# Norm factors computed with tokens on partitions, a reordered end of two projections, and a folded pool bias and scale

## The chip, the cores and the metric

The kernel runs on one core of a Trainium2 chip. The metric is the device time of one execution in microseconds. TensorE is called PE here, its weight load PEld, VectorE DVE, ScalarE ACT, GpSimd POOL; SP issues the weight DMAs.

## The reference

Two decoder layers run over 272 tokens (16 learned meta tokens and 256 positions) of width 2048. Layer 0 mixes with a Mamba-2 scan, layer 1 with causal pooling; each is followed by a SwiGLU FFN of hidden width 5632, and every sub-layer stands between two RMSNorms:

```python
def rmsnorm(x, w):
    y = x * lax.rsqrt(jnp.mean(x * x, axis=-1, keepdims=True) + EPS)
    return y * w

for i in range(DEPTH):                      # DEPTH = 2
    u = rmsnorm(h, norm_w[i, 0])
    mix = ssd_mixer(u, ...) if i % 2 == 0 else pool_mixer(u, ...)
    h = h + rmsnorm(mix, norm_w[i, 1])
    f = (silu(u2 @ w_gate[i]) * (u2 @ w_up[i])) @ w_down[i]   # u2 = rmsnorm(h, norm_w[i, 2])
    h = h + rmsnorm(f, norm_w[i, 3])
return h[:, N_META:]

def pool_mixer(u, w_group, b, scale):       # four channel groups, windows 2, 4, 8, 16
    mixed = trailing_mean(u, window of the group) - u
    return (einsum('blgc,gcd->blgd', mixed, w_group) + b) * scale
```

## The kernel before

**Panels and steps.** Activations lie with features on partitions and tokens along the free axis, so that a weight block is the stationary operand and 272 (in layer 1's FFN 256) tokens stream. A weight matrix is worked off as panels of 512 or 768 output columns; a panel has 4 or 6 PSUM accumulators (`acc_*`, six buffers in turn) and is cut into steps of one or two blocks of 128 rows. Each fp32 weight is split: ACT casts it to `whi` (L162), DVE subtracts to get `wlo` (L175), and every block takes three matmuls (L275 to L277: hi by hi, hi by lo, lo by hi). `run_stream` goes through the steps in program order: at each step it emits the cast of the step after next and, after the third accumulator, its subtraction. Within a step all accumulators take their matmuls one after another, so the four accumulators of a panel end within its last step. A panel with `late` set puts its last subtraction behind its last accumulator.

**Junctions.** Between the sub-layers stands a row of norm factors, 1/sqrt(mean square), one number per token. `SumSq` squares the tiles of the sub-layer's output `part` on ACT, adds the squares on DVE into `ssum` or multiplies them by a matrix of ones on PE (L640: the sum over the features, repeated on all 128 partitions), and `row` takes the square root on ACT (L660). `recip` inverts the 128x272 row on DVE (L664). Then the `Producer` makes the sixteen new tiles of `h` and of the next operand `uu`: for each tile a scaled copy of `part` (`tmp`, L707), the sum with `h` (L716), `uu` hi on ACT (L717), a square, and `uu` lo on DVE (L727). It runs two tiles ahead of the matmuls and its `hook` sets in the subtraction of the next weight step. `warm` issues matmuls whose result nobody reads.

There are three such places, called A, B and C below:

- **A** (about 771 to 783 us): from the SSD output projection (panel `oB3`, accumulators `acc_oB`) to the gate panel `g0_0_0` of the first FFN (`acc_g`). PE also transposes the last eight tiles of the input there (L896, L898), which ACT copies into `h` (L899).
- **B** (about 1578 to 1618): from the down projection `d0_1_3` (`acc_d`) to layer 1's pool mixer. The sixteen tiles feed four panels of four blocks: two with tokens on the output partitions (`acc_tok`, copied to `zt`), then two like the others (`acc_pool`, copied to `part` by L1013).
- **C** (about 1615 to 1640): the second norm of the pool mixer. The factor row `rb2` of the mixer's input is inverted (L664), read back through PE transposes as columns `rt` (L1020 to L1023), multiplied into six tiles of a band matrix on ACT (L1039), and into the window sums on DVE (L1057, L1062, L1069). Band matmuls give `acc_mix` (L1046 to L1049). Sixteen output tiles get bias and scale (`tile_out`, L1030 on ACT and L1032 on DVE), are squared and summed on PE, and give the factor row of the junction to the second FFN.

The order of everything here is the order in which the code emits it; each engine works off its own instructions in that order, and there is no planner at these places.

Of the kernel before, what the change touches and what calls it, by code (L numbers as in the profile page):

```python
# [15 lines left out]
P = 128  # L16
D = 2048
# [14 lines left out]
class Panel:  # L32
    def __init__(self, name, w, nk, rhs, n, evac, after=None, ncols=512, ku=4, ks=2, dup=False,
                 need=(), pre=None, prestep=None, mm=None, func=None, late=False, lazy=False, nm=None, both=None):
        self.name, self.w, self.nk, self.rhs, self.n = name, w, nk, rhs, n
        self.evac, self.after, self.ncols, self.ku, self.ks, self.dup = evac, after, ncols, ku, ks, dup
        self.func, self.late, self.lazy, self.both = func, late, lazy, both
# [30 lines left out]
def trunk_kernel(ctx: ExitStack, tc: tile.TileContext, x, meta, norm_w, w_in, conv_w, conv_b,  # L68
# [171 lines left out]

    def run_stream():
        for si, s in enumerate(steps):
# [11 lines left out]
            if p.prestep is not None:  # L254
                p.prestep(s["k0"], s["ks"], lambda si=si: emit_lo(si + 2))
            for m in range(p.nm):
                if p.mm is not None:
                    p.mm(s, m, first, last)
                else:
                    if first:  # L260
                        p.accs.append(acc_tile(p.name))
                    a = p.accs[m]
                    for j in range(s["ks"]):
                        k = s["k0"] + j
                        xh, xl = p.rhs(k)
                        wh = s["hi"][:, j, m * P:(m + 1) * P]
                        wl = s["lo"][:, j, m * P:(m + 1) * P]
                        st, en = k == 0, k == p.nk - 1
                        if p.both is not None:

                            nc.tensor.matmul(a[:, :2 * p.n].rearrange("p (a c) -> p a c", c=p.n), lhsT=wh,  # L271
                                             rhs=p.both(k), start=st, stop=False)
                            nc.tensor.matmul(a[:, p.n:2 * p.n], lhsT=wl, rhs=xh, start=False, stop=en)  # L273
                            continue
                        nc.tensor.matmul(a[:, :p.n], lhsT=wh, rhs=xh, start=st, stop=False)  # L275
                        nc.tensor.matmul(a[:, :p.n], lhsT=wh, rhs=xl, start=False, stop=False)  # L276
                        nc.tensor.matmul(a[:, :p.n], lhsT=wl, rhs=xh, start=False, stop=en)  # L277
# [4 lines left out]
                if last and p.mm is None:  # L282
# [324 lines left out]
    class SumSq:  # L607


        def __init__(self, n):  # L610
            self.n, self.acc, self.pend, self.adds, self.bank = n, None, [], [], None
# [21 lines left out]
        def push(self, keep=0, stop=False):  # L633

            while len(self.pend) > keep:
                sq = self.pend.pop(0)
                first = self.bank is None
                if first:
                    self.bank = bank("pt")
                nc.tensor.matmul(self.bank[:, :self.n], lhsT=ones[:, 0:P], rhs=sq, start=first,  # L640
# [21 lines left out]

    def recip(dst, n):
        nc.vector.reciprocal(out=dst[:, :n], in_=dst[:, :n])  # L664

    def evac_sum(pi, n):

        def evac(m, a):
            k = pi * 4 + m
            o = part[:, k, T - n:T]  # L670
            if k == 0:
                F["ss"] = SumSq(n)
            nc.vector.tensor_tensor(out=o, in0=o, in1=a[:, :n], op=ALU.add)
            F["ss"].late()
            if pi == 3:
                F["ss"].pe(o)
                if m == 0:
                    F["ss"].push_acc()
# [7 lines left out]
    def norm_row(dst):  # L686
        n = F["ss"].n
        F["ss"].row(dst)
        F["ss"].warm(WARM)
        recip(dst, n)  # L690

    class Producer:


        def __init__(self, order, l1, w1, l2, w2, n, on_pe):
            self.order, self.n, self.on_pe = order, n, on_pe
            self.a, self.b = (l1, w1), (l2, w2)
            self.ss = SumSq(n)
            self.tmps, self.made = {}, 0

        def tmp(self, i):
            if i >= KD:
# [3 lines left out]
            self.tmps[i] = t  # L706
            nc.vector.scalar_tensor_tensor(out=t, in0=part[:, k, T - n:T], scalar=nw(*self.a, k),  # L707
                                           in1=rb[:, :n], op0=ALU.mult, op1=ALU.mult)

        def make(self, i, hook):  # L710
# [5 lines left out]
            nc.vector.tensor_tensor(out=hk, in0=hk, in1=self.tmps.pop(i), op=ALU.add)  # L716
# [121 lines left out]
    def ffn(layer, n, junction, tail):  # L838
# [6 lines left out]
        for half, widths in enumerate(((6, 4, 4, 4, 6), (4, 4, 4, 4, 4))):  # L845
# [14 lines left out]
            for pi in range(4):  # L860
                w = w_down[layer][h0 * P:c0 * P, pi * 512:(pi + 1) * 512]
                if tail is None:
# [3 lines left out]
                    elif half == 1 and pi == 3:  # L866
# [9 lines left out]
                                late=half == 1 and pi == 3, pre=sqrt_table if half == 1 and pi == 3 else None))  # L876
# [474 lines left out]
```

## Time and profile before

| | us |
|---|---|
| median of 3 runs | 2399.9 (2398.23 to 2399.99) |
| the profiled execution, its own time | 2399.69 |
| its span | 2397.6 |
| PE busy | 2364.3 (99%), 16660 matmuls |
| DVE busy | 1447.8 (60%) |
| ACT busy | 1180.2 (49%) |
| DMA | 418.37 MB, 174 GB/s |

How to read it: PE is busy nearly always, so time moves only where PE stands idle, where it does work that a change takes away or adds, or where its clock is low. A busy PE includes its matmuls at either clock.

### The profile page before, as it was taken

The numbers are of one execution on the slowest core, as the hardware profiler recorded it, in microseconds if no ns is written. First come the engines' busy times: TensorE is split into PE (matmuls) and PEld (weight loads), VectorE is DVE, ScalarE is ACT, GpSimd is POOL, SyncE is SP. The second block draws the span as 40 slices with busy tenths as digits, with TensorE's granted clock in tenths as the row PEclk, the third lists the DMA queues.
The fourth block names the chain that finished last, engine by engine and source line by source line (L and its number), as shares of the span: only waits on it lengthen the run. The fifth ranks groups of instructions, "written<-read, shape, count | busy, mean of one in ns | idle before, by whom it ended". The sixth has DMA issues, their size and how long they took to land.

```text
span 2397.6 us, 39491 instructions
## 1 busy us (share of the span) xinstructions
PE 2364.3 (99%) x16660; PEld 2219.0 (93%) x16660; DVE 1447.8 (60%) x1927; ACT 1180.2 (49%) x1605; POOL 13.8 (1%) x38
## 2 busy tenths in 40 slices
PE   7999999999999999999999999999999999999998
PEld 7999999999999999999999999988888888888886
DVE  5878867647865855454445454578666554556655
ACT  6656565445654644443344443456544444444443
POOL 0000000000000000000000000010000000000000
PEclk9999999999999999999999999999999999999999
DMA  6555555555554555565555555433665655565554
GB/s 190 170 165 182 177 167 176 170 176 178 176 178 158 147 189 175 163 189 176 176 176 173 179 176 176 167 120 106 191 195 173 192 195 192 177 199 187 197 189 141
DMA packets 203825, 418.37 MB, mean 174 GB/s; under 512 B 9920, under 2 KB 10416, under 8 KB 203504
## 3 DMA queue, kind: packets, MB, share of 16 engines
q1 hardware_dynamic: 203216, 415.07, 53.9%
q8 instruction: 130, 2.13, 0.4%
q10 hardware_dynamic: 432, 0.79, 0.1%
q14 instruction: 47, 0.39, 0.0%
HBM read 413.66 MB, written 2.17 MB: 173 GB/s over the span
## 4 chain that ended last, share of the span: by engine, by line
PE 96%; DVE 2%; ACT 1%; issue 0%; DMA 0%; SPq 0%; DVEq 0%; ACTq 0%
PE acc_g L271 7%; PE acc_u L271 7%; PE acc_g L276 4%; PE acc_g L277 4%; PE acc_d L277 4%; PE acc_g L275 4%; PE acc_u L275 4%; PE acc_u L277 4%; PE acc_u L276 4%; PE acc_d L276 4%; PE acc_d L275 4%; PE acc_g L273 3%; PE acc_u L273 3%; PE acc_z L275 3%; PE acc_z L277 3%; PE acc_z L276 3%
## 5 line engine op out<-in xcount | busy, mean ns | idle before, releaser
L175 DVE TENSOR_TENSOR wlo<-raw,whi 128x1024 fp32r<-128x1024 f32 (+2 forms) x804 | 936.9, 1167 | 772.3 <-ACT whi L162 767.7
L162 ACT CAST whi<-raw 128x1024 fp32r<-128x1024 f32 (+2 forms) x800 | 803.1, 1005 | 951.6 <-PE acc_u L276 149.3
L271 PE MATMUL acc_g<-uu,whi 128*128 128x512 f32 x704 | 248.5, 396 | 2.5 <-DVE uu L727 1.3
L271 PE MATMUL acc_u<-uu,whi 128*128 128x512 f32 x704 | 247.0, 394 | 0.2 <-DVE g L789 0.2
L275 PE MATMUL acc_g<-uu,whi 128*128 128x272 f32 x704 | 204.8, 291 | 0.9 <-ACT uu L717 0.9
L277 PE MATMUL acc_g<-uu,wlo 128*128 128x272 f32 x704 | 203.8, 289 | 0.0
L276 PE MATMUL acc_g<-uu,whi 128*128 128x272 f32 x704 | 203.5, 289 | 0.1
L277 PE MATMUL acc_u<-uu,wlo 128*128 128x272 f32 x704 | 203.2, 289 | 0.0
L277 PE MATMUL acc_d<-hidhi,wlo 128*128 128x272 f32 x704 | 203.2, 289 | 0.0
L275 PE MATMUL acc_u<-uu,whi 128*128 128x272 f32 x704 | 203.1, 288 | 0.0
L276 PE MATMUL acc_u<-uu,whi 128*128 128x272 f32 x704 | 202.7, 288 | 0.0
L275 PE MATMUL acc_d<-hidhi,whi 128*128 128x272 f32 x704 | 202.3, 287 | 0.0
L276 PE MATMUL acc_d<-hidlo,whi 128*128 128x272 f32 x704 | 202.2, 287 | 0.0
L273 PE MATMUL acc_g<-uu,wlo 128*128 128x256 f32 x704 | 197.2, 280 | 0.7 <-DVE wlo L175 0.7
L273 PE MATMUL acc_u<-uu,wlo 128*128 128x256 f32 x704 | 197.0, 280 | 0.0
L271 PEld LDWEIGHTS acc_g<-uu,whi 128*128 128x128 f32 x704 | 132.1, 188 | 34.9 <-DVE ups L815 1.9
L271 PEld LDWEIGHTS acc_u<-uu,whi 128*128 128x128 f32 x704 | 132.1, 188 | 32.0 <-DVE g L789 0.6
L275 PE MATMUL acc_z<-uu,whi 128*128 128x272 f32 x512 | 150.7, 294 | 0.0
L275 PE MATMUL acc_x<-uu,whi 128*128 128x272 f32 x512 | 150.2, 293 | 0.0
L277 PE MATMUL acc_x<-uu,wlo 128*128 128x272 f32 x512 | 147.6, 288 | 0.0
L277 PE MATMUL acc_z<-uu,wlo 128*128 128x272 f32 x512 | 147.6, 288 | 0.0
L276 PE MATMUL acc_x<-uu,whi 128*128 128x272 f32 x512 | 147.4, 288 | 0.0
(384 smaller groups left out, 5250.0 us busy)
## 6 DMA issues: line engine op xcount, KB each, us to landing
raw<-in_ffn_w_down_dram SPq DMA_DIRECT2D x88, 1024.0 KB, 5.0
raw<-in_ssd_w_in_dram SPq DMA_DIRECT2D x76, 1024.0 KB, 5.3
raw<-in_ffn_w_gate_dram SPq DMA_DIRECT2D x64, 1024.0 KB, 5.2
raw<-in_ffn_w_up_dram SPq DMA_DIRECT2D x64, 1024.0 KB, 5.2
raw<-in_ssd_w_out_dram SPq DMA_DIRECT2D x32, 1024.0 KB, 5.1
raw<-in_ffn_w_gate_dram SPq DMA_DIRECT2D x32, 768.0 KB, 4.5
raw<-in_ffn_w_up_dram SPq DMA_DIRECT2D x32, 768.0 KB, 4.5
bc<-cs_dram SPq DMA_DIRECT2D x32, 272.0 KB, 6.0
```

The lines of the kernel that those rows point to most:

```text
L162: nc.scalar.copy(out=s["hi"], in_=raw)
L175: nc.vector.tensor_tensor(out=s["lo"][:, :, sl], in0=raw, in1=s["hi"].bitcast(F32)[:, :, sl], op=ALU.subtract)
L271: nc.tensor.matmul(a[:, :2 * p.n].rearrange("p (a c) -> p a c", c=p.n), lhsT=wh, rhs=p.both(k), start=st, stop=False)
L273: nc.tensor.matmul(a[:, p.n:2 * p.n], lhsT=wl, rhs=xh, start=False, stop=en)
L275: nc.tensor.matmul(a[:, :p.n], lhsT=wh, rhs=xh, start=st, stop=False)
L276: nc.tensor.matmul(a[:, :p.n], lhsT=wh, rhs=xl, start=False, stop=False)
L277: nc.tensor.matmul(a[:, :p.n], lhsT=wl, rhs=xh, start=False, stop=en)
```

## The change

1. **Norm factors with tokens on partitions.** With `cols` set, a tile of squares is the stationary operand and one column of ones streams: three matmuls 128x1 (blocks of 128, 128 and 16 tokens, or two for 256 tokens) in place of one of 128x272. `factor_cols` takes the square root and the reciprocal of 128x3 numbers and multiplies them into an identity, one block on ACT and the others on DVE; `factor_row` multiplies these diagonal blocks by ones on PE, which puts the row on all partitions (`acc_row`, in PSUM), and ACT copies it to SBUF. The first two `tmp` read it in PSUM. In `norm_row` two warm matmuls stand ahead of the row and four behind it. At A this whole helper now stands ahead of the transposes, and it had no warm matmuls there before. The factor rows `rb2` of both FFNs keep the old way.
2. **The last two steps by accumulator.** Panels `oB3` and `d0_1_3` have `major` set: in their last two steps each accumulator takes all its twelve matmuls before the next begins. Their last step emits neither a cast nor a subtraction any more; the `hook` of the `Producer` does both. The squares of the first three accumulators go to DVE sums.
3. **The pool bias and scale.** `evac_pool` applies the scale when it copies. Squares are taken straight from `acc_mix` with scale and bias in the activation; the bias is added in `tmp`, and the norm weight moves from `tmp` to the addition to `h`. The factors `rt` come from `factor_cols`, the transposes go.

```diff
             if p.prestep is not None:
-                p.prestep(s["k0"], s["ks"], lambda si=si: emit_lo(si + 2))
+                p.prestep(s["k0"], s["ks"], lambda si=si: (emit_hi(si + 2), emit_lo(si + 2)))
...
+                elif p.major and s["k0"] >= p.nk - 4:
+
+                    if s["k0"] == p.nk - 4:
+                        if m == 0:
+                            emit_hi(si + 2)
+                            emit_lo(si + 2)
+                        for t in (s, steps[si + 1]):
+                            panel_mm(p, t, m)
+                        p.evac(m, p.accs[m])
...
-                if m == 0:
+                if m == 0 and not (p.major and last):
                     emit_hi(si + 1 + LOOK)
...
-                if not p.lazy and m == (p.nm - 1 if p.late and last else min(2, p.nm - 1)):
+                if not p.lazy and not (p.major and last) and m == (p.nm - 1 if p.late and last else min(2, p.nm - 1)):
                     emit_lo(si + 1 + LOOK)
...
+                if self.cols:
+                    for i, (t0, w, _) in enumerate(self.blocks):
+                        nc.tensor.matmul(self.bank[:, i:i + 1], lhsT=sq[:, t0:t0 + w], rhs=ones[:, 0:1],
...
+        def factor_cols(self, rs):
...
+            self.push(stop=True)
+            nb = len(self.blocks)
+            nc.scalar.activation(out=rs[:, 0:nb], in_=self.bank[:, 0:nb], func=AF.Sqrt, scale=1.0 / D, bias=eps)
+            nc.vector.reciprocal(out=rs[:, 0:nb], in_=rs[:, 0:nb])
+            self.dg = F["pool"].tile([P, T], F32, name="sq", bufs=6)
+            for i, (t0, _, w) in enumerate(self.blocks):
+                o, c = self.dg[0:w, t0:t0 + w], rs[0:w, i:i + 1]
+                if i == 1:
+                    nc.scalar.activation(out=o, in_=ident[0:w, 0:w], func=AF.Copy, scale=c)
+                else:
+                    nc.vector.tensor_scalar(out=o, in0=ident[0:w, 0:w], scalar1=c, scalar2=None, op0=ALU.mult)
+
+        def factor_row(self, dst):
+
+            b = acc_tile("row")
+            for t0, _, w in self.blocks:
+                nc.tensor.matmul(b[:, t0:t0 + w], lhsT=ones[0:w, 0:P], rhs=self.dg[0:w, t0:t0 + w], start=True,
+                                 stop=True)
+            nc.scalar.copy(out=dst[:, :self.n], in_=b[:, :self.n])
+            return b
...
     def norm_row(dst):
-        n = F["ss"].n
-        F["ss"].row(dst)
-        F["ss"].warm(WARM)
-        recip(dst, n)
+
+        rs = F["pool"].tile([P, 3], F32, name="rsc")
+        F["ss"].factor_cols(rs)
+        F["ss"].warm(2)
+        b = F["ss"].factor_row(dst)
+        F["ss"].warm(WARM - 3)
+        return b
...
             if gi == 3 and k0 == 2:
-                G["prod"].ss.row(rb2)
-                recip(rb2, T)
+                G["prod"].ss.factor_cols(G["rt"])
+                for b in G["band"]:
+                    for i in range(3):
+                        nc.scalar.activation(out=b[:, i, :], in_=b[:, i, :], func=AF.Copy, scale=G["rt"][:, i:i + 1])
...
-            nc.scalar.copy(out=part[:, g * 4 + m, :], in_=a[:, :T])
+            k = g * 4 + m
+            nc.scalar.activation(out=part[:, k, :], in_=a[:, :T], func=AF.Copy, scale=col(PSC, k))
+            if g == 0 and m == 1:
+                G["prod"].ss.factor_row(rb2)
```

The order on PE at place A, before: behind the last matmuls of `acc_oB` come the sums over the squares, then the transposes of the input.

```order
L277 MATMUL acc_oB_8317<-yhi,wlo 128x272
L640 MATMUL pt<-ssum,ones 128x272
L640 MATMUL pt<-sq,ones 128x272 x4
L896 MATMUL acc_h<-ident,mr 128x16
L898 MATMUL acc_h<-ident,xr 128x128 x2
```

The same place after; `py` are warm matmuls.

```order
L257 MATMUL acc_oB_8317<-yhi,wlo 128x272
L655 MATMUL pt<-ones,ssum 128x1 x3
L655 MATMUL pt<-ones,sq 128x1 x3
L666 MATMUL py<-ones,ident 128x272 x2
L704 MATMUL acc_row<-sq,ones 128x128 x2
L704 MATMUL acc_row<-sq,ones 128x16
L666 MATMUL py<-ones,ident 128x272 x4
L953 MATMUL acc_h<-ident,mr 128x16
L955 MATMUL acc_h<-ident,xr 128x128 x2
```

The sums have become narrow, and six warm matmuls and the row now stand ahead of the transposes.

DVE at place B, before, from the last addition to `part` to the third tile of the `Producer`:

```order
L673 TENSOR_TENSOR part<-part,acc_d_1_3_16524 128x272
L175 TENSOR_TENSOR wlo<-raw,whi 128x1024
L664 RECIPROCAL rb<-rb 128x272
L707 SCALAR_TENSOR_TENSOR tmp<-part,pv,rb 128x272
...
L716 TENSOR_TENSOR h<-h,tmp 128x272
L707 SCALAR_TENSOR_TENSOR tmp<-part,pv,rb 128x272
L626 TENSOR_TENSOR ssum<-ssum,sq 128x272
L727 SCALAR_TENSOR_TENSOR uu<-h,pv,uu 128x272
```

And after:

```order
L175 TENSOR_TENSOR wlo<-raw,whi 128x1024
L719 TENSOR_TENSOR part<-part,acc_d_1_3_16546 128x272
L639 TENSOR_TENSOR ssum<-ssum,sq 128x272
L691 RECIPROCAL rsc<-rsc 128x3
L698 TENSOR_SCALAR sq<-ident,rsc 128x128
L698 TENSOR_SCALAR sq<-ident,rsc 16x16
L761 SCALAR_TENSOR_TENSOR tmp<-part,pv,acc_row 128x272
...
L761 SCALAR_TENSOR_TENSOR tmp<-part,pv,rb 128x272
L639 TENSOR_TENSOR ssum<-ssum,sq 128x272
L175 TENSOR_TENSOR wlo<-raw,whi 128x1024
L785 SCALAR_TENSOR_TENSOR uu<-h,pv,uu 128x272
```

One subtraction moved ahead of the last addition, the other from behind it into the third tile (at A the same, with 128x768); its cast stands on ACT behind that tile's `uu`.

ACT at the start of place C, after (before, the second cast and the four copies of `acc_pool` stood ahead of the bands, and the window sums read a row that DVE had inverted itself):

```order
L690 ACTIVATE rt<-pt,eps 128x3
L696 ACTIVATE sq<-ident,rt 128x128
L1042 ACTIVATE band_16835<-band_16835,rt 128x144 x3
L1042 ACTIVATE band_16843<-band_16843,rt 128x144 x3
L162 CAST whi<-raw 128x768
L1069 ACTIVATE part<-acc_pool_17188,pv 128x272
L1069 ACTIVATE part<-acc_pool_17197,pv 128x272
L706 COPY rb_90<-acc_row 128x272
```

The copy of the row that the window sums on DVE read is the last of these.

## Rows read from the trace of the kernel before

**Rows 1.** the page, busy time of the engines, share of the span and instructions

```profile
PE 2364.3 (99%) x16660; PEld 2219.0 (93%) x16660; DVE 1447.8 (60%) x1927; ACT 1180.2 (49%) x1605; POOL 13.8 (1%) x38
```

**Rows 2.** windows: stretch, its length, busy us of each engine, clock, DMA share, GB/s

```profile
782.00:795.00 13.00, 13.00 (x102) 12.92 (x102) 13.00 (x28) 9.48 (x19) 0.00 (x0) 0.99 0.41 121
...
1587.00:1600.00 13.00, 12.97 (x57) 8.94 (x57) 12.81 (x31) 9.66 (x20) 0.00 (x0) 1.00 0.18 49
1600.00:1618.00 18.00, 17.02 (x111) 14.59 (x111) 16.34 (x31) 13.70 (x30) 0.00 (x0) 1.00 0.32 98
```

**Rows 3.** timeline of PE at A: start, us, line, operation, count, idle before

```profile
771.47 2.00 PE L640 MATMUL pt<-sq,ones 128*128 128x272 f32 x8
...
773.39 0.23 PE L896 MATMUL acc_h<-ident,mr 16*128 16x16 f32 x1
...
783.00 0.29 PE L277 MATMUL acc_g<-uu,wlo 128*128 128x272 f32 x1
```

**Rows 4.** timeline of ACT at A, same columns

```profile
771.68 0.43 ACT L630 ACTIVATE sq<-part 128x272 f32<-128x272 f32 x1 [0.32 <-DVE part L673]
...
773.50 0.49 ACT L660 ACTIVATE rb<-pt,eps 128x272 f32<-128x272 f32 x1 [1.39 <-PE pt L640]
...
774.03 4.10 ACT L899 COPY h<-acc_h 128x272 f32<-128x272 f32 x8
...
778.02 0.52 ACT L717 ACTIVATE uu<-h,pv 128x272 fp32r<-128x272 f32 x1
...
780.91 0.52 ACT L717 ACTIVATE uu<-h,pv 128x272 fp32r<-128x272 f32 x1 [0.60 <-DVE h L716]
```

**Rows 5.** timeline of DVE at A

```profile
771.21 0.44 DVE L673 TENSOR_TENSOR part<-part,acc_oB 128x272 f32<-128x272 f32 x1 [0.31 <-PE acc_oB L277]
...
775.91 0.50 DVE L707 SCALAR_TENSOR_TENSOR tmp<-part,pv,rb 128x272 f32<-128x272 f32 x1
...
783.09 0.95 DVE L175 TENSOR_TENSOR wlo<-raw,whi 128x768 fp32r<-128x768 f32 x1
```

**Rows 6.** timeline at the kernel's start, where small factors are made (ACT, DVE)

```profile
11.43 0.30 ACT L1273 ACTIVATE rs<-rs,eps 128x3 f32<-128x3 f32 x1 [0.39 <-DVE rs L1272]
...
11.97 0.35 DVE L1284 TENSOR_SCALAR xt<-xt,rs 128x256 f32<-128x256 f32 x1
```

**Rows 7.** timeline of PE in the band matmuls of C

```profile
1621.19 0.29 PE L1048 MATMUL acc_mix<-band,zt 128*128 128x16 f32 x2
...
1621.34 0.38 PE L1049 MATMUL acc_mix<-band,zt 128*128 128x16 f32 x2
...
1621.56 0.45 PE L1046 MATMUL acc_mix<-band,zt 128*128 128x112 f32 x2
```

**Rows 8.** timeline of DVE at B

```profile
1581.55 1.85 DVE L664 RECIPROCAL rb<-rb 128x272 f32<-128x272 f32 x1 [1.24 <-ACT rb L660]
...
1588.04 0.49 DVE L727 SCALAR_TENSOR_TENSOR uu<-h,pv,uu 128x272 fp32r<-128x272 f32 x1
```

**Rows 9.** timeline of ACT at B

```profile
1587.39 0.52 ACT L717 ACTIVATE uu<-h,pv 128x272 fp32r<-128x272 f32 x1 [0.60 <-DVE h L716]
...
1589.67 1.04 ACT L162 CAST whi<-raw 128x1024 fp32r<-128x1024 f32 x1
...
1611.96 1.24 ACT L1013 COPY part<-acc_pool 128x272 f32<-128x272 f32 x4
```

**Rows 10.** timeline of ACT at C

```profile
1619.79 1.94 ACT L1039 ACTIVATE band<-band,rt 128x144 f32<-128x144 f32 x6
```

**Rows 11.** timeline of DVE at C

```profile
1618.90 1.29 DVE L1057 TENSOR_TENSOR part<-part,rb 128x1088 f32<-128x1088 f32 x1
...
1631.53 0.41 DVE L1032 TENSOR_SCALAR part<-part,pv,bs 128x256 f32<-128x256 f32 x1
...
1637.57 0.49 DVE L707 SCALAR_TENSOR_TENSOR tmp<-part,pv,rb 128x256 f32<-128x256 f32 x1
```

**Rows 12.** windows, a stretch of A, columns as in rows 2

```profile
779.00:780.00 1.00, 0.90 (x5) 0.87 (x5) 0.85 (x3) 0.53 (x2) 0.00 (x0) 0.50 0.00 0
```

More of the change, by code (lines that the diff above doesn't have):

```diff
@@ L639, in push @@
                     self.bank = bank("pt")
+                if self.cols:
+                    for i, (t0, w, _) in enumerate(self.blocks):
+                        nc.tensor.matmul(self.bank[:, i:i + 1], lhsT=sq[:, t0:t0 + w], rhs=ones[:, 0:1],
+                                         start=first and i == 0,
+                                         stop=stop and not self.pend and i == len(self.blocks) - 1)
+                    continue
                 nc.tensor.matmul(self.bank[:, :self.n], lhsT=ones[:, 0:P], rhs=sq, start=first,
@@ L706, in tmp @@
             self.tmps[i] = t
+            row = self.row if i < 2 else rb
+            if self.bias is not None:
+                nc.vector.scalar_tensor_tensor(out=t, in0=part[:, k, T - n:T], scalar=self.bias[:, k:k + 1],
+                                               in1=row[:, :n], op0=ALU.add, op1=ALU.mult)
+                return
             nc.vector.scalar_tensor_tensor(out=t, in0=part[:, k, T - n:T], scalar=nw(*self.a, k),
-                                           in1=rb[:, :n], op0=ALU.mult, op1=ALU.mult)
+                                           in1=row[:, :n], op0=ALU.mult, op1=ALU.mult)
         def make(self, i, hook):
@@ L875, in ffn @@
                                 need=((nt - widths[-1], un),) if pi == 0 else (),
[L876 removed]
+                                major=half == 1 and pi == 3, pre=sqrt_table if half == 1 and pi == 3 else None))
     def evac_partial(pi, n):
@@ L1017, in pool_out @@
         f = G["pool"]
[L1018 to L1039 removed]
+        ss = SumSq(SEQ, cols=True)
+        F["ss"] = ss
+        bs = G["bs"]
         def mix(gi, j):
@@ L1071, in end, with scaled, square, square_sum @@
             return v[:, j, NM:T]
-        bands(0)
+        def scaled(k, y, eng):
+            o = part[:, k, NM:T]
+            if eng == "act":
+                nc.scalar.activation(out=o, in_=y, func=AF.Copy, scale=col(PSC, k))
+            else:
+                nc.vector.tensor_scalar(out=o, in0=y, scalar1=col(PSC, k), scalar2=None, op0=ALU.mult)
+        def square(k, y):
+            ss.pe(y, col(PSC, k), bs[:, k:k + 1])
+        def square_sum(k, o):
+            ss.dve(o, 1.0, bs[:, k:k + 1])
+        ys = [mix(0, j) for j in range(4)]
         sums(1)
-        ys = [mix(0, j) for j in range(4)]
-        bands(1)
         for j in range(4):
-            ss.pe(tile_out(12 + j, ys[j], "act"))
-        ys = [mix(1, j) for j in range(4)]
-        ss.push(keep=2)
+            square(12 + j, ys[j])
+            scaled(12 + j, ys[j], "act")
         for j in range(4):
-            o = end(1, j)
-            ss.pe(tile_out(4 + j, o, "dve"))
+            square_sum(4 + j, end(1, j))
+        ys = []
+        for j in range(4):
+            ys.append(mix(1, j))
+            ss.push(keep=3 - j)
         sums(0)
-        ss.push(keep=2)
         for j in range(4):
-            ss.pe(tile_out(8 + j, ys[j], "act"))
+            square(8 + j, ys[j])
+            scaled(8 + j, ys[j], "dve")
+        ss.late()
+        for j in range(4):
             o = end(0, j)
-            ss.pe(tile_out(j, o, "dve"))
-            ss.push(keep=2)
+            if j < 2:
+                square_sum(j, o)
+                ss.push(keep=2 - j)
+            else:
+                if j == 2:
+                    ss.late()
+                    ss.push_acc()
+                ss.pe(o, 1.0, bs[:, j:j + 1])
+                ss.push(keep=2)
     pw = pool_w[0]
```

115 lines of the change are left out of this document (51 added, 64 removed).

## The prediction

> **What bounds the kernel now.** The page comes first: PE is busy 99% of the span [rows 1]. There is nothing to win off PE except where PE waits, so the windows by stage are read next. In the long panels PE is packed: 13.00 of 13 us behind place A [rows 2]. A delay that a junction hands to such a stretch is not made up in it, it goes into the end. In the tile production of B, DVE is busy 12.81 of 13 us beside a PE with 12.97 [rows 2]: and later, in 1600 to 1618, 16.34 of 18 beside 17.02 [rows 2]: there whoever of the two is late sets the pace. The timelines of A, B and C then tell which step stands last at each place.
>
> At A the reader sees two chains side by side. On DVE and ACT: last addition 771.21 [rows 5], its square 771.68, the square root 773.50 [rows 4], the reciprocal, the first `tmp` 775.91 [rows 5]. On PE: four sums over squares, then from 773.39 the transposes [rows 3], whose copies occupy ACT from 774.03 for 4.10 us; the first `uu` at 778.02 follows right behind them, without any idle time printed [rows 4]. So at A the transposes are last, not the factor row. At B and C nothing of that kind is there, and the chain of the row is last.
>
> **The change part by part.** Unless another place is named, durations are of the profiled execution, 2399.69 us, 0.2 below the median of the runs shown.
>
> *Narrow sums.* Before, PE ends its sums with four wide ones over squares in 1.92 us, 0.48 each (773.39 - 771.47) [rows 3]. After, one tile of squares costs three matmuls of one column. The trace has none. The nearest are the 16-column ones, which come in pairs of passes too: 0.15 from L1048 to L1049 and 0.22 from there to the next [rows 7]. The first may still be riding on weights loaded earlier, the second pays them; since each narrow sum brings new weights, I take 0.23, and keep 0.15 as the other end. Two tiles (`ssum` and the last square) make 6 x 0.23 = 1.4 us, against the end of the four wide ones. The Trainium skill ("TensorE: Matmul & The Clock Gate", Part 1, on the 56 ns gap) puts the floor between starts of small matmuls at about 25 ns. By that figure the six would take an estimated 0.3 us; the weight loads seen here speak against it.
>
> *The moved subtraction.* The accumulators now end twice as far apart, and the subtraction of 0.95 (A) or 1.23 (B, half again as many columns) lies between third and last addition. It nearly fits; I take the last addition 0.1 late at A and 0.35 at B (bounds: nothing, and the whole subtraction).
>
> *Square root to `tmp`.* Before 775.91 - 773.50 = 2.41, of which 1.85 is the reciprocal [rows 4, 5, 8]. After: the start of the kernel has the same small steps, 0.54 from a 128x3 square root over its reciprocal to the scaling [rows 6]; the diagonal blocks are less than the 0.35 of a 128x256 scaling there, so 0.35 for two; the row is three fp32 matmuls of 0.23; 0.2 for the way to DVE, an estimate. Sum 1.8, so 0.6 is won. At the square root itself we are later by 0.1 + (0.47 + 0.43 + 1.4 + 0.1 = 2.4 from addition to root, before 2.29) = 0.2 at A and 0.45 at B. Net: `tmp` 0.4 early at A, 0.15 early at B.
>
> *A: the transposes.* This gain meets the wrong chain. Transposes now wait for the row (773.7 + 0.54 + 0.35 + 0.7 = 775.3) and four warm matmuls at 0.48, 1.9 us: 777.2 in place of 773.39, **3.8 late**. The copies and the first `uu` go with them. Behind that the second step's cast and subtraction, which the old order had finished in the gap, now stand in the third tile: `uu` at 780.91, 0.43 later the cast of 0.82, then the 0.95 subtraction [rows 4, 5], done at 783.15 plus 3.8, when PE needed it at 783.00 [rows 3]. What PE does in its first step is covered until then, at either clock. **A costs 3.8 + 0.25 = 4.05** (3.0 with sums at 0.15 and no late addition, 4.5 with the subtraction fully in the way), and PE is packed behind it [rows 2].
>
> *B.* `tmp` starts 0.15 early. The third tile then waits: cast 0.43 behind its `uu` (1587.39), 1.04 long [rows 9], then the subtraction, 1.22 with an overlap of 0.09 into the next (an estimate); `uu` lo comes 1587.39 + 0.43 + 1.04 + 1.13 + 0.05 = 1590.04 in place of 1588.04 [rows 8], 2.0 late. Scaling in `evac_pool`: four copies took 1.24 [rows 9]; a scaled `uu` takes 0.52 [rows 9], some 0.43 apiece at speed, so 0.48 more, ahead of a `uu` on ACT. DVE, nearly full at B, can take back little. It reaches the last tile 2.0 - 0.15 + 0.48 = 2.3 late (1.7 to 2.8).
>
> *C.* The window sums started at 1618.90, right behind the long reciprocal, which then began near 1617.0 (1618.90 - 1.85) [rows 11, 8]. The new short one is at 1617.0 + 2.3 = 1619.3; from there ACT does a diagonal (0.5 with the reciprocal), the bands 1.94 [rows 10], a cast 0.8, two scaled copies 0.86 and the copy of the row 0.4: 1623.8, **4.9 late**. DVE's work from there to 1631.53 + 0.41 was 13.0 [rows 11]. It loses four scalings of 0.41, gains five additions of about 0.34 and no longer stalls behind each of its own results: 12.4, an estimate. It ends 4.3 late, at 1636.25. The tail from there to `tmp` was 5.6 (to 1637.57 [rows 11]), nearly all of it PE and ACT working off sixteen squares; now one square 0.5, two narrow matmuls 0.55, root to `tmp` 1.55: 2.6, at 1638.85. **C ends 1.3 late at full clock.**
>
> *The clock at C.* At A, the granted clock is 0.50, that is 1.2 GHz, in 779 to 780 [rows 12], some six us after the last wide sum (773.39 [rows 3]), with only transposes and a wait between. At C, PE now has about six us of narrow matmuls between the last band matmul (near 1631) and the two warm ones (1636.8), where sixteen wide sums lay before. I expect the clock to have fallen there: two warm matmuls and the row take twice as long, 0.9 of it and 0.5 not hidden by the root. **C then costs 2.6.** The Trainium skill (same page, Part 4) says that transposes don't count as PE work for the clock the same way; the low clock after the transposes at A agrees, and it leaves the sums above as they are.
>
> Sum: 4.05 + 2.6 = 6.65, from 2399.69 **2406.3**. The other edits change nothing that is last: the bias in `tmp` and the weight in `h` add about 0.06 per tile on DVE in a panel where PE has more to do, and wide sums in the two FFN rows stay.
>
> **The rivals.** *The clock holds at C* (the narrow matmuls keep it up): 4.05 + 1.3, **2405.0**. For it: B and C hold 2.4 GHz before. Against it: [rows 12].
>
> *Cover at the lower ends*: narrow sums at 0.15 save 0.5 at A and at B, DVE's idle time in B swallows 1.3 of the 2.3, and the clock holds: 3.5 + (1.3 - 0.5 - 1.3) = 3.0, **2402.7**. For it: DVE is idle 0.19 + 1.66 us in the two stretches of B [rows 2]. Against it: much of that is DVE waiting for ACT, whose work moves along with it. The 25 ns floor of the Trainium skill's page would act this way too.
>
> *Faster: each reciprocal is paid back in full.* Four long ones, at A, B, the factor of the mixer and C, become short: 4 x (1.85 - 0.2) = 6.6, **2393.1**. It needs the row's chain last at all four places, and it decides from the point where the 3.8 us at A and the 2.0 at B are covered. Against it: the `uu` at 778.02 follows the copies and not the row [rows 4].
>
> *Worse*: the low clock also stretches the first gate step at C, or the subtraction at B lies fully in the way: another 2 to 3, **2409**.
>
> **How the numbers follow.** A measurement of this kernel tells about 0.2% (4.8 us) from no change. Forecast 2406.3 with 0.42; clock holds 0.16; cover 0.24; faster 0.07; worse 0.11. Slower by over 0.2% means above 2404.5: the forecast, worse, and half of the second, 0.61. Within: the cover case and the other half, 0.32. Faster: 0.07. The range leaves out the faster case, the lower end of cover and the upper end of worse: 2401.5 to 2409.
>
> **What would show it.** The changed profile proves A right if the transposes start near 777 and the first `uu` near 782, and wrong if `uu` comes before 780. B is right if `uu` lo of the third tile comes about two us after its `ssum`, behind the cast; C if the window sums wait for the copy of `rb2` on ACT until about 1628 (A's 4.05 included), and the clock between the last band matmul and the gate panel reads 0.50 somewhere. Narrow sums should stand 0.15 to 0.23 apart. The prediction fails if the second step's subtraction is not waited for, or if PE has idle time behind A that absorbs the delay.

## The result, and the profile after

The changed kernel takes 2412.89 us (2412.15 to 2416.6) against 2399.07 (2397.67 to 2399.99) for the kernel before, run beside it: a ratio of 1.0060, 95% interval 1.0045 to 1.0075. It is slower, as forecast, but by 13.8 us and not by 6.6, and above the range. The profiled execution is one of 2412.24 us, with a span of 2410.2.

The page, busy time (before: [rows 1]):

```profile
PE 2373.3 (98%) x16723; PEld 2226.5 (92%) x16723; DVE 1445.6 (60%) x1941; ACT 1180.5 (49%) x1607; POOL 13.0 (1%) x37
```

DVE has 2 us less work and PE 9 us more. The two traces, cut at the same instructions (us):

| stretch | before | after | more | forecast |
|---|---|---|---|---|
| A: last matmul of `acc_oB` to the first `wlo` matmul of the second gate step | 12.12 | 17.85 | 5.73 | 4.05 |
| from there to the last addition at B | 795.74 | 796.32 | 0.58 | 0.35 |
| B: to `uu` lo of the last of the sixteen tiles | 36.37 | 39.14 | 2.77 | 1.95 |
| to the window sums | 3.79 | 6.14 | 2.35 | 2.6 |
| C: to the end of DVE's work | 13.04 | 13.42 | 0.38 | -0.6 |
| to `tmp` | 5.63 | 6.70 | 1.07 | -1.7 |
| sum | 866.69 | 879.57 | 12.88 | 6.65 |

(This execution reached A 0.81 us sooner, from its first 22 us, where the programs are alike, and lost 0.5 behind `tmp`; so its span is 12.6 longer.) A and the last two stretches of C hold 5.4 us of the error of 6.2, B 0.8. Timelines at A, PE then ACT and DVE (before: [rows 3 to 5]); in brackets the idle time before and what ended it:

```profile
770.07 0.29 PE L257 MATMUL acc_oB<-yhi,wlo 128*128 128x272 f32 x1
...
772.65 1.50 PE L666 MATMUL py<-ones,ident 128*128 128x272 f32 x4
773.95 1.59 PE L704 MATMUL acc_row<-sq,ones 128*128 128x128 f32 x6
775.47 2.71 PE L666 MATMUL py<-ones,ident 128*128 128x272 f32 x8
778.12 0.23 PE L953 MATMUL acc_h<-ident,mr 16*128 16x16 f32 x1
...
787.92 0.39 PE L257 MATMUL acc_g<-uu,wlo 128*128 128x272 f32 x1
...
782.74 0.53 ACT L775 ACTIVATE uu<-h,pv 128x272 fp32r<-128x272 f32 x1
...
776.00 0.50 DVE L761 SCALAR_TENSOR_TENSOR tmp<-part,pv,acc_row 128x272 f32<-128x272 f32 x1 [2.25 <-ACT rb L706]
```

Windows of the same stretch (the column before the last two is the granted clock):

```profile
773.00:777.00 4.00, 4.00 (x14) 3.13 (x13) 1.49 (x6) 0.88 (x3) 0.00 (x0) 0.57 0.00 0
777.00:782.00 5.00, 5.00 (x29) 3.13 (x27) 0.45 (x2) 2.39 (x7) 0.00 (x0) 1.00 0.02 3
```

The transposes wait for row and warm matmuls, as forecast. Most of that work ran at a granted clock of 0.50, that is 1.2 GHz (from 773.3 to 776.7), which was not forecast. DVE at B, the first `tmp` and the third tile:

```profile
1589.38 0.50 DVE L761 SCALAR_TENSOR_TENSOR tmp<-part,pv,acc_row 128x272 f32<-128x272 f32 x1 [1.53 <-ACT rb L706]
...
1594.82 1.23 DVE L175 TENSOR_TENSOR wlo<-raw,whi 128x1024 fp32r<-128x1024 f32 x1 [0.77 <-ACT whi L162]
1595.96 0.50 DVE L785 SCALAR_TENSOR_TENSOR uu<-h,pv,uu 128x272 fp32r<-128x272 f32 x1
```

And C, DVE then PE (before: [rows 11]):

```profile
1629.52 1.29 DVE L1096 TENSOR_TENSOR part<-part,rb 128x1088 f32<-128x1088 f32 x1 [3.60 <-ACT rb L706]
...
1641.66 0.95 DVE L639 TENSOR_TENSOR ssum<-ssum,sq 128x256 f32<-128x256 f32 x2
1642.53 0.41 DVE L1108 SCALAR_TENSOR_TENSOR part<-win,part 128x256 f32<-128x256 f32 x1
...
1649.64 0.48 DVE L758 SCALAR_TENSOR_TENSOR tmp<-part,bs,acc_row 128x256 f32<-128x256 f32 x1 [2.58 <-ACT rb L706]
...
1642.67 1.02 PE L655 MATMUL pt<-ones,ssum 128*128 128x1 f32 x4 [3.55 <-DVE ssum L639]
1643.55 2.70 PE L655 MATMUL pt<-ones,sq 128*128 128x1 f32 x12
1646.11 2.16 PE L666 MATMUL py<-ones,ident 128*128 128x272 f32 x4
1648.06 1.06 PE L704 MATMUL acc_row<-sq,ones 128*128 128x128 f32 x4
```

```profile
1640.00:1644.00 4.00, 1.33 (x7) 1.33 (x7) 2.81 (x8) 1.81 (x4) 0.00 (x0) 0.54 0.00 0
1644.00:1648.00 4.00, 4.00 (x15) 3.60 (x16) 0.45 (x2) 0.66 (x2) 0.00 (x0) 0.50 0.00 0
```

PE stands idle for 3.55 us until DVE has `ssum`, then works off all that is queued behind it at the low clock: narrow sums, two warm matmuls and the row take 6.4 us. (Each matmul of a sum stands in these traces as two records, called passes below: the `x16` of four tiles are eight matmuls.) The clock reads 0.50 from 1641 to 1650.

### The profile page after: what moved, and what is told of

Its sections match the earlier page's. It is cut to its first block, busy times and chain, and to the rows that moved or that the text cites. A ratio compares the mean times of both kernels' runs of the same rounds, so it can differ in the third digit from the quotient of the medians.

```text
span 2410.2 us, 39633 instructions
## 1 busy us (share of the span) xinstructions
PE 2373.3 (98%) x16723; PEld 2226.5 (92%) x16723; DVE 1445.6 (60%) x1941; ACT 1180.5 (49%) x1607; POOL 13.0 (1%) x37
## 4 chain that ended last, share of the span: by engine, by line
PE 95%; DVE 3%; ACT 1%; issue 1%; DMA 0%; SPq 0%; DVEq 0%; ACTq 0%
PE acc_g L251 7%; PE acc_u L251 7%; PE acc_g L257 4%; PE acc_g L256 4%; PE acc_g L255 4%; PE acc_u L255 4%; PE acc_u L257 4%; PE acc_d L257 4%; PE acc_u L256 4%; PE acc_d L256 4%; PE acc_d L255 4%; PE acc_g L253 3%; PE acc_u L253 3%; PE acc_z L255 3%; PE acc_z L257 3%; PE acc_z L256 3%
```

## The experiments

Each total is told against the kernel before, timed in the same batch (medians 2399.4 to 2400.14). The times of one kernel lie 1 to 5 us apart, so smaller differences between two edits are read from stretches of the profiled executions, one for each kernel. Stretches at A are counted from the last matmul of `acc_oB`.

**a_nowarm: no warm matmuls at A.**

```diff
-            row = norm_row(rb)
+            row = norm_row(rb, warm=l1 == 1)   # A: neither of the two warm() calls
```

> The changed kernel without the six warm matmuls at A (two ahead of the row, four behind it); B and C keep theirs. Theory 1 (the transposes are last at A, and the warm matmuls stand in their way): the transposes start some 2.8 us earlier against the last matmul of acc_oB (the four warm ones behind the row took 2.65 us), the first uu follows by the same 2.8, and the total falls from 2412.2 to about 2409.5. Rival (the warm matmuls hold the clock up and pay for themselves): the clock falls earlier, transposes and the first gate step run longer, and the total stays within 1 us of 2412.2. If the factor row were last at A, the first uu would not move at all.

The transposes start 2.86 earlier (5.19 in place of 8.05), but the first `uu` comes only 0.44 earlier, and the total stays 13.4 above before. The rival holds: the clock was at 0.50 from 774.2 to 787.8, so that the copies on ACT wait for each transposed tile, in place of standing packed as in [rows 4]:

```profile
775.89 0.69 PE L957 MATMUL acc_h<-ident,xr 128*128 128x128 f32 x2
...
777.44 0.39 ACT L958 COPY h<-acc_h 128x272 f32<-128x272 f32 x1 [0.45 <-PE acc_h L957]
```

**a_first: two transposed tiles ahead of the row, six behind it, no warm matmuls at A.**

```diff
+            row = norm_row(rb, mid=(lambda: late_h(2)) if todo else None)   # between factor_cols and factor_row
+            late_h(8)
```

> The changed kernel without the warm matmuls at A, and with two of the eight transposed tiles ahead of the factor row and six behind it. Theory 1 (order on PE): the transposes start right behind the narrow sums as in the kernel before, the copies on ACT again end some 4.1 us later, and the first uu comes 4.5 to 5 us earlier than in the changed kernel: total about 2407.7. Rival (the subtraction of the second weight step, now in the third tile, takes over): the first uu moves by 4.5 or more, but the first matmul with wlo of the second block by only some 2.5, and the total is about 2409.7.

The transposes start at 2.65 (before 2.51), the first `uu` comes at 9.81 in place of 12.67: 2.9 earlier and not 4.5, since the clock fell at 775.9 and the copies again wait 0.45 each. The second step's `wlo` matmul gains 2.7, the total is 11.6 above before. These are the rival's figures for matmul and total, but not its mechanism: `uu` itself came only 2.9 earlier. What the order is worth without the low clock, the next run shows.

**b_hook: cast and subtraction of the second step behind the last accumulator again.**

```diff
-                if m == 0 and not (p.major and last):
+                if m == 0:
                     emit_hi(si + 1 + LOOK)
...
-                if not p.lazy and not (p.major and last) and m == (p.nm - 1 if p.late and last else min(2, p.nm - 1)):
+                if not p.lazy and m == (p.nm - 1 if (p.late or p.major) and last else min(2, p.nm - 1)):
                     emit_lo(si + 1 + LOOK)
```

> The changed kernel, with the cast and the subtraction of the second step of the next panel again behind the last accumulator of oB3 and d0_1_3 (the two steps still go accumulator by accumulator). Theory 1 (the 2.0 us of the third tile at B are handed on, and the wait of 0.55 at A too): at B the uu lo of the third tile comes 1.6 us earlier against the last addition (2.0 less some 0.4 by which the subtraction now delays the short reciprocal), the last tile of B 1.6 earlier too, and with 0.3 at A the total falls by about 1.9, to 2410.3. Rival (DVE takes the time back within B's sixteen tiles anyway): the third tile is earlier, the last tile within 0.5 of where it was, and the total within 0.7 of 2412.2.

From the first `tmp` to `uu` lo of the third tile it takes 4.54 in place of 6.58 (before 4.60): the 2.0 of the forecast. From the last addition to the last tile: 38.15, with a stretch at the low clock behind the last addition. a_nowarm, with a like stretch, has 40.07, so 1.9 arrives there. The total is 12.5 above before; the 1.3 less than the 13.8 of the changed kernel lie within the spread. In this profile the clock stayed at 1.00 through A, with the same warm matmuls, row and transposes as in the changed kernel:

```profile
770.88 0.29 PE L257 MATMUL acc_oB<-yhi,wlo 128*128 128x272 f32 x1
...
777.49 0.23 PE L953 MATMUL acc_h<-ident,mr 16*128 16x16 f32 x1
...
785.73 0.29 PE L257 MATMUL acc_g<-uu,wlo 128*128 128x272 f32 x1
...
782.12 0.53 ACT L775 ACTIVATE uu<-h,pv 128x272 fp32r<-128x272 f32 x1
```

```profile
773.00:777.00 4.00, 4.00 (x23) 3.25 (x23) 2.38 (x7) 1.05 (x3) 0.00 (x0) 1.00 0.49 116
777.00:782.00 5.00, 4.80 (x27) 2.81 (x25) 0.44 (x2) 2.86 (x8) 0.00 (x0) 1.00 0.17 68
```

Here transposes come 4.10 later than before (6.61 against 2.51) and the first `uu` 4.10 (11.24 against 7.14). The second step's `wlo` matmul stands at 14.85.

**warm_ac: more warm matmuls.**

```diff
+        if F["ss"].n == T:
+            F["ss"].warm(2)              # ahead of the narrow sums at A and B
...
                 ss.push(keep=2 - j)
+                if j == 1:
+                    ss.warm(6)           # at the end of C
```

> The changed kernel with two more warm matmuls ahead of the narrow sums at A and B, and six (2.9 us at the high clock) in the idle time of PE at the end of C (1639.1 to 1642.7 in the changed kernel). Theory 1 (the clock fell because PE stood idle or had only narrow matmuls, and the low clock is what made C's tail long): the granted clock stays at 1.00 from the last band matmul to the gate panel; at C the sixteen last passes of the narrow sums take 1.8 us less, the two warm ones 1.1 and the row 0.5 less, so that tmp comes some 3 us earlier against DVE's end; at A warm, row and warm take up to 1.8 less. Total 2407 to 2409. Rival (narrow matmuls bring the clock down whatever stands between, or the clock is not what is last): clock and tail as they were, total 2412 or up to 1 more.

At A the clock stayed at 1.00 and the first `uu` came at 11.23; but b_hook did so without them, so that proves nothing. It shows the price of the moved cast and subtraction at the high clock: PE waits for both, and its `wlo` matmul comes at 16.42, in b_hook at 14.85.

```profile
786.27 0.39 PE L255 MATMUL acc_g<-uu,whi 128*128 128x272 f32 x1 [0.67 <-ACT whi L162]
...
787.27 0.40 PE L257 MATMUL acc_g<-uu,wlo 128*128 128x272 f32 x1 [0.48 <-DVE wlo L175]
```

At C the aim was missed: the clock had fallen at 1635.2, still in the mixing matmuls, and the six warm ones then took 4.4 us (1642.31 to 1646.68) ahead of `ssum`. Window sums to `tmp` became 21.19; total 12.0 above before. But the warm ones brought the clock back to 1.00 at 1645.4, and so the run prices the low clock in the tail:

```profile
1646.68 0.50 PE L655 MATMUL pt<-ones,ssum 128*128 128x1 f32 x4
1647.05 1.48 PE L655 MATMUL pt<-ones,sq 128*128 128x1 f32 x12
...
1650.63 0.48 DVE L760 SCALAR_TENSOR_TENSOR tmp<-part,bs,acc_row 128x256 f32<-128x256 f32 x1 [1.29 <-ACT rb L706]
```

From the first matmul with `ssum` to `tmp` it takes 3.95 here and 6.97 in the changed kernel: 3.0 more for the same instructions.

**nomajor: the second part undone** (`late=` in place of `major=` in both panels).

> The changed kernel with the second part undone: the last two steps of oB3 and d0_1_3 go block by block again, with cast and subtraction of the second step where they were, the squares on DVE sums as in the changed kernel. Theory 1 (the reordered end costs more than it gives): the last addition at B comes 0.5 earlier, the third tile's uu lo about 2 us earlier against it, A gains about 0.4; total some 2.5 below the changed kernel, about 10.5 above the kernel before. Rival (with the accumulators ending close together the additions and squares crowd and the root comes later by what the order had gained): from the last matmul of acc_oB to the root of A 0.5 or more later, total within 1 of the changed kernel.

The last addition at B came 0.28 earlier and the third tile as in b_hook (4.54 from `tmp`). A gained nothing in this profile (clock 0.50 from 774.5 to 781.3), and C lost 2.8 to a low clock from 1634.6 on. Total 11.9 above before: 1.9 less than the changed kernel, where some 2.5 were expected, but within the spread and so not shown.

**d_copy: the row's copy behind the first two `tmp`.**

```diff
             row = self.row if i < 2 else rb
+            if i == 2:
+                nc.scalar.copy(out=rb[:, :n], in_=self.row[:, :n])   # no longer in factor_row
```

> The changed kernel with the copy of the row from PSUM to SBUF emitted behind the first two tmp of a junction, not ahead of them. Theory 1 (the first tmp waits for ACT's copy though it reads PSUM, 0.4 us at each place): from the last addition to tmp at B 0.4 less (4.7 in place of 5.14 at the high clock), at C from the root to tmp 0.4 less; A is held by its transposes; total 0.8 below the changed kernel, which alone can't be told from no change, so the stretches decide. Rival (the wait is for PE's row, and the copy only ended it by chance): the stretches stay within 0.1.

Root to `tmp` is 1.92 at A against 2.33 in b_hook, both at the high clock, and 2.95 at C against 3.36, both at the low one: 0.41 at each. The rival fell: the first `tmp` did wait for a copy that it doesn't read. But the third `tmp` now waits for the copy, and the third tile with it:

```profile
775.92 0.50 DVE L764 SCALAR_TENSOR_TENSOR tmp<-part,pv,acc_row 128x272 f32<-128x272 f32 x1 [0.99 <-PE acc_row L704]
...
784.74 0.50 DVE L764 SCALAR_TENSOR_TENSOR tmp<-part,pv,rb 128x272 f32<-128x272 f32 x1 [0.86 <-ACT rb L759]
...
787.34 0.39 PE L255 MATMUL acc_g<-uu,whi 128*128 128x272 f32 x1 [1.35 <-ACT whi L162]
```

The total is 16.0 above before, worse than without the edit. Not all of that is the edit's: at C the clock fell at 1639.2 in this execution, among the mixing matmuls, and DVE's work there took 15.18.

**c_row: the row ahead of the bands at C.**

```diff
-            if g == 0 and m == 1:
+            if g == 0 and m == 0:       # ahead of the scaled copies; the six bands now follow these
                 G["prod"].ss.factor_row(rb2)
```

> The changed kernel with the factor row rb2 formed behind the first accumulator of the last pool panel, ahead of its scaled copies, and the six bands scaled on ACT behind these copies. Theory 1 (the window sums wait for a copy that stands behind bands, cast and two scaled copies on ACT, and DVE's work is what C ends on): the window sums start 2.3 us earlier against the last tile of uu lo (3.8 in place of 6.1), the end of DVE's work and tmp follow by 2.0 or more, total about 11 above the kernel before. Rival (the mixing matmuls, now 1 to 1.5 later behind the bands, and the squares behind them become last): the window sums come 2.3 earlier, DVE then waits for squares or for acc_mix, and tmp gains 1 or less.

The window sums came 2.15 earlier (3.99 behind the last tile), and DVE then waited for squares of `acc_mix`, which waited for the bands:

```profile
1632.80 0.45 PE L1082 MATMUL acc_mix<-band,zt 128*128 128x112 f32 x2 [1.28 <-ACT band L1124]
...
1640.01 0.48 DVE L1114 TENSOR_SCALAR part<-acc_mix,pv 128x256 f32<-128x256 f32 x1 [4.03 <-ACT sq L643]
```

DVE's work took 19.13 in place of 13.42, total 17.5 above before. The rival holds, and more strongly than priced: at C the chain bands, mixing, squares stands as late as the window sums.

**old_rows: wide sums, long reciprocal and the old place of the transposes at the three junctions.**

```diff
+        F["ss"].row(dst)
+        if mid is not None:
+            mid()                        # the transposes, at A
+        else:
+            F["ss"].warm(WARM)
+        recip(dst, n)
```

> The changed kernel with the first part undone at the three junctions: wide sums, one 128x272 square root and the long reciprocal at A, B and C, the transposes at A between root and reciprocal and no warm matmuls there; the factor rt of the mixer keeps the new way, parts 2 and 3 stay. Theory 1 (at C the narrow sums let the clock fall, and the sums and warm matmuls at the low clock make the tail): the granted clock stays at 1.00 from the mixing matmuls to the gate panel, and from the window sums to tmp at C it takes about 17.4 us, against 20.1 in the changed kernel and 18.7 in the kernel before. Theory 2 (order at A): the first uu comes 7.2 after the last matmul of acc_oB, as before (7.14), against 12.67. Total about 4.5 us above the kernel before. Rival (squares and sums have the same price in either form, and the long reciprocal comes on top): C's stretch stays at 20 or more, the total 7 to 8 above the kernel before.

The first `uu` at A is as before (6.97): theory 2 holds. That the `wlo` matmul is too (12.15 against 12.12) is luck: c_pe_wide below, with the same code at A and the clock at 1.00, also has 12.15, with PE waiting for the subtraction, which stays moved here; p3_pe, with the old code and the clock at 1.00, has 10.74. At C theory 1 fell: 19.30 and not 17.4, with PE idle for 3.45 us and the clock at 0.50 from 1636.1 to 1642.9, wide sums or not:

```profile
1637.49 1.22 PE L659 MATMUL pt<-ssum,ones 128*128 128x256 f32 x2 [3.45 <-DVE ssum L639]
```

Total 6.6 above before, between the 4.5 of the theories and the 7 to 8 of the rival. The squares that DVE sums were left as a suspect.

**c_pe and c_pe_wide: every square at C summed on PE as it comes**, in the changed kernel and in old_rows.

```diff
-            square_sum(4 + j, end(1, j))
+            ss.pe(end(1, j), 1.0, bs[:, 4 + j:5 + j])
+            ss.push(keep=2)
...
-        ss.late()
...
+            ss.pe(end(0, j), 1.0, bs[:, j:j + 1])
+            ss.push(keep=2)
```

> The changed kernel, with every square at C summed on PE as it comes (narrow sums, in the order of the tiles) and none on DVE. Theory 1 (C's tail is long because the last eight squares stand behind DVE's additions, while PE waits idle for ssum for some 3.5 us, and then works them off at the low clock): DVE loses five additions, so from the window sums to the end of its work 11.3 in place of 13.42; from there to the root 1.0 to 1.9 in place of 3.34; window sums to tmp 15 to 16.5 against 20.12; total some 4 below the changed kernel, about 9 above the kernel before. Rival (PE's narrow sums in series, 0.45 a tile for sixteen tiles beside the mixing matmuls, are last, at the low clock): PE is packed up to the root, window sums to tmp 19 or more.

> The kernel with wide sums and the long reciprocal at the three junctions (old_rows), and with every square at C summed on PE as in c_pe. Theory 1 (the low clock at C follows the idle time and the narrow sums of PE): the granted clock stays at 1.00 at C, window sums to tmp about 15.5 to 16.5 against 19.30 in old_rows; total about 3 below old_rows, 3.5 above the kernel before. Rival (the mixing matmuls with their 16 and 112 columns bring the clock down whatever the sums are): the clock is at 0.50 somewhere between the mixing matmuls and the gate panel, as in old_rows, and the stretch stays above 17.5.

DVE's work falls to 11.7 in both. With wide sums the tail shrinks too, window sums to `tmp` 15.89, total 2.5 above before. With narrow ones it is 19.73, total 12.9 above: the rival. PE was packed in both, in the same order. Windows and sums of c_pe:

```profile
1638.00:1642.00 4.00, 4.00 (x38) 4.00 (x37) 3.37 (x7) 2.83 (x6) 0.00 (x0) 1.00 0.00 0
1642.00:1646.00 4.00, 4.00 (x21) 4.00 (x21) 1.29 (x4) 1.70 (x4) 0.00 (x0) 0.51 0.00 0
```

```profile
1637.93 10.00 PE L655 MATMUL pt<-ones,sq 128*128 128x1 f32 x64
```

And of c_pe_wide:

```profile
1630.00:1634.00 4.00, 4.00 (x23) 3.59 (x23) 3.36 (x6) 2.76 (x6) 0.00 (x0) 1.00 0.00 0
1634.00:1638.00 4.00, 4.00 (x20) 3.51 (x19) 1.81 (x6) 2.08 (x5) 0.00 (x0) 1.00 0.00 0
```

```profile
1630.43 7.15 PE L659 MATMUL pt<-sq,ones 128*128 128x256 f32 x32
```

Sixteen tiles cost 7.15 us wide. Narrow, 37 passes (one weight load each) fit into 4 us at the high clock, so 64 would take some 7; they took 10.0, because the clock fell among them. The two forms cost about the same, and in these two runs only the wide one kept the clock.

c_pe_wide also shows the moved subtraction at A, with the clock at 1.00: PE waits for it, and this matmul stands 12.15 behind the last one of `acc_oB`.

```profile
783.20 0.39 PE L257 MATMUL acc_g<-uu,wlo 128*128 128x272 f32 x1 [0.47 <-DVE wlo L175]
```

**p3_pe: the kernel before with the third part alone**, squares on PE, `rt` through transposes.

> The kernel before, with the third part alone (scale in the copy of acc_pool, squares straight from acc_mix, bias in tmp, norm weight in the addition to h), all squares summed wide on PE as they come, the factor rt through transposes as before. Theory 1 (this part gains where its squares don't wait for DVE's sums): A and B as before, 0.35 later by the scaled copies, DVE's work at C some 1.8 shorter, window sums to tmp 15.5 to 17 against 18.67; total 1.5 to 3 below the kernel before. Rival (ACT, which has two activations on acc_mix per tile either way, ends C): the stretch stays between 18 and 19, the total within 1 of the kernel before.

Total 0.5 above before (ratio 1.0003, 0.9994 to 1.0011), window sums to `tmp` 18.64: the rival. The mixing matmuls start 1.76 behind the window sums, and what DVE saves it waits for their squares (14.46 to the end of its work). At A the clock stayed at 1.00, and the `wlo` matmul of the second step comes 10.74 behind the last one of `acc_oB`:

```profile
770.46 0.29 PE L277 MATMUL acc_oB<-yhi,wlo 128*128 128x272 f32 x1
...
781.20 0.29 PE L277 MATMUL acc_g<-uu,wlo 128*128 128x272 f32 x1
```

**best: A and B as before, at C c_pe_wide with the row copied by DVE and four window tiles summed there.**

> A and B as in the kernel before (old order of the last two steps, wide sums, long reciprocal); at C the changed kernel's short way to rt and the bands, but the row rb2 copied by DVE, which is idle there, wide sums, the first four window tiles summed on DVE and all others on PE as they come. Theory 1 (what c_pe_wide showed adds up with the old A and B): from the last tile of uu lo to tmp at C 20.0 to 21.5 against 22.46 in the kernel before (3.79 + 18.67), A and B within 0.5 of it, the clock at C at 1.00; total 1 to 2.5 below the kernel before, which needs many runs to be told from it. Rival (PE's eight mixing matmuls and sixteen sums are packed and set the end, so an earlier window sum gives nothing): 22.0 or more, total within 0.5 of the kernel before.

The last tile to `tmp` takes 21.41 (before 22.46), the clock at C stays at 1.00, the total is 2399.48 against 2400.14, ratio 0.9999 (0.9990 to 1.0008): the stretch is 1.05 shorter, the total can't be told from before.

## Why the prediction was wrong in size

**A, the order: right.** At the high clock the transposes and the first `uu` come 4.10 late (b_hook), forecast 3.8. p3_pe has A's old code and also ran at 1.00: its `wlo` matmul stands at 10.74, b_hook's at 14.85, again 4.11.

**A, the moved subtraction: mis-sized.** The step read 0.25 from the old trace, where PE "needed it at 783.00". That PE was itself late by 1.4, through the low clock of [rows 12] (12.12 against 10.74 in p3_pe, same code). Against a PE at the high clock the step costs 1.57 (warm_ac less b_hook), in the old order 1.41 (c_pe_wide less p3_pe).

**A, the clock: missing.** The forecast let it fall at C alone. In the changed kernel the warm matmuls and the row ran mostly at 0.50: the transposes start at 8.05 and not at 6.61 as in b_hook and warm_ac, and first `uu` and `wlo` matmul keep that distance from warm_ac (1.44 and 1.43). The low clock of the first gate step (783.5 to 786.9) costs nothing on top, as the prediction had it. Together: order 4.11, subtraction 1.57, clock 1.43, less the 1.38 that the low clock had cost the kernel before, 5.73.

**B: mechanism right.** The third tile is 2.0 late (1.98), the scaled copies cost 0.37 (1.61 for four in place of 1.24; forecast 0.48). Root to `tmp` was put at 1.8; at A it is 1.92 without the wait for the copy (d_copy) and 2.3 with it, and at B 2.76, where it was 2.41 before, so that `tmp` came 0.44 later behind the last addition and not 0.15 earlier. The "0.2 for the way to DVE" left out the wait for the copy, 0.41; the rest at B stays open. The last addition came 0.58 late (0.35), of which nomajor ties 0.28 to the order; the other 0.30 also shows in p3_pe, whose code there is the old one, and stays open.

**C, the window sums: right**, 2.35 for 2.6.

**C, DVE's work: wrong sign.** Five additions were taken at 0.34; from start to start they take 0.43 (1.26 for three, 0.87 for two). The forecast then took 0.7 off (13.0 less 1.6 plus 1.7 is 13.1, put at 12.4) because DVE "no longer stalls". No row showed that: DVE had been idle 0.54 us in this stretch before (busy 12.50 of 13.04) and is idle 0.57 now (12.85 of 13.42).

**C, the tail: the step that failed most.** "One square 0.5, two narrow matmuls 0.55, root to `tmp` 1.55: 2.6" counted only the last tile; with the 1.3 for the low clock the forecast was 3.9, and 6.70 was measured. `ssum` stands in PE's order ahead of the last squares and comes from DVE's last additions, so four tiles, 16 passes, are left when it arrives. Counted from the end of DVE's work, 0.27 behind the first of them, warm_ac's 3.95 at the high clock are 3.7: the queue costs 1.1 more than 2.6. The low clock adds 3.0 and not 1.3, since it holds for the 16 passes (3.44 us in place of 1.71) as for the two warm matmuls and the row.

Neither the order nor the form of the sums alone explains it (window sums to `tmp`):

| | last window tiles through `ssum` | all squares on PE |
|---|---|---|
| narrow sums, short reciprocal | 20.12 (clock falls) | 19.73 (falls) |
| wide sums, long reciprocal | 19.30 (falls) | 15.89 (holds) |

The 20.12 stands in a_nowarm, a_first and b_hook too, whose code at C is the same. That the clock at C goes with the form of the sums doesn't rest on c_pe alone. In the four profiles with wide sums and no wait for `ssum` (before, p3_pe, c_pe_wide, best) the clock reads 1.00 from 1612 to 1660. In all nine with narrow sums it fell between window sums and `tmp`, in five of them (b_hook at 1635.3, warm_ac at 1635.2, nomajor at 1634.6, d_copy at 1639.2, c_pe at 1642.1) while PE was busy without a gap; in old_rows it fell while PE waited for `ssum`. Why it falls at one moment and not at another stays open.

**Two sums of the prediction** don't close as printed: at A 783.15 less 783.00 is 0.15 and not 0.25, at C 1.3, 0.9 and 0.5 make 2.7 and not 2.6. They cancel in the 6.65.

**The rivals.** "The clock holds at C" failed, it fell at 1640.3. "Cover" failed: narrow sums took 0.22 each and not 0.15, and B swallowed nothing, its stretch grew by 2.77. "Faster" failed, at A as argued, where the transposes were last; elsewhere the short reciprocal wins little between root and `tmp` even at the high clock: 2.33 (b_hook at A) for 2.41, 2.07 (warm_ac at C) for 2.30, where the rival needed 1.65 each time. "Worse" had the right idea with too small a price.

## What to carry to other kernels

When a sum is made narrow, look at what else the wide one did: in the runs here wide sums that PE did not have to wait for went with a clock of 2.4 GHz, at the same cost, and the short reciprocal won less than the low clock lost. Count a tail from the operand that comes last in the engine's order, and cost everything queued behind it. Before an edit is priced against a wait in a trace, see whether the low clock made that wait.

## What the hardware showed

A narrow pass, one column against 128 columns of new weights, takes 0.11 us at 2.4 GHz (37 in 4.00 us, c_pe) and 0.22 at 1.2 GHz (2.70 for 12, changed kernel). By the Trainium skill ("TensorE: Matmul & The Clock Gate", Part 2, on LDWEIGHTS: P / 1.2 ns for P columns) loading 128 columns takes an estimated 107 ns. The pass at the high clock agrees with it; the one at the low clock, twice as long, doesn't.

In c_pe PE was busy with narrow passes for 4.00 of 4 us at 1.00 (1638 to 1642), went on with them, and the clock fell to 0.50 at 1642.1. The same code at the same place ran at 1.00 in one execution and at 0.50 in another: A in the kernel before and in p3_pe differ by 1.4 us with this, so one profile doesn't settle a step of that size.

The Trainium skill (same page, Part 4) says that transposes don't count as PE work for the clock the same way. In b_hook it stayed at 1.00 through all 24 matmuls of the transposes, in p3_pe through these and the first gate step behind them, in a_first it fell among them. So the low clock after the transposes of the kernel before, which the prediction took as agreeing, doesn't settle it, and neither do these runs.
